# A three-block fp32 kernel on one core: the last stage's three products as half products, gated in SBUF

## The chip, the core and the metric

The kernel runs on one core of a Trainium2 chip. The metric is the device time of one execution in microseconds, from the runs of the kernel before: a median of 3840.6 over three runs (3840.37, 3840.6 and 3845.19).

## What is computed

Three residual blocks follow each other on 1024 rows of width 1024, all in fp32. The change lies at the end of the third one, and in the pools of the second and third. What matters of the reference:

```python
def hybrid_layer(x, w_in, ..., w_pa, w_pb, w_o):
    ...
    g_a = jax.nn.sigmoid(gate_a + b_gate[:D_MODEL])
    g_b = jax.nn.sigmoid(gate_b + b_gate[D_MODEL:])
    m = g_a * (y_a @ w_pa) + g_b * (y_b @ w_pb)
    return x + rms_norm_3(m @ w_o, g_post)
```

y_a is 1024 x 2048, y_b is 1024 x 1024, and all three results are 1024 x 1024. So the stage has three matrix products with inner sizes 2048, 1024 and 1024.

## The kernel before

Every fp32 operand is split into a high part, rounded by a copy on ACT (L183), and a low part, the difference taken on DVE (L184). A product of two operands is three matmuls: high by high, high by low, low by high (`mm3`, L266). A matmul is 128x128 by 128x512, and eight PSUM banks of 128x512 hold the results.

Two stages of the kernel already use fewer products. `Seven` (L1701) makes the third block's gates and first branch with seven products of quarter blocks in place of eight. `Second` (L2448) does the second block's second feed-forward product the same way: m = 1 to 7 are products of 512-column halves, each with an operand that is one block or a sum or difference of two. The A operands come ready from HBM (`hS`), since the stage ahead makes their sums; the B operands are weight blocks, summed on POOL (L2485). A product of one step is 24 matmuls (two k tiles, three matmuls each, four row tiles). After the last step each product's four 128x512 results are added to or taken from one or two quadrants of `xm`; products 1, 3, 4 and 5 go to SBUF by an ACT copy (L2513) and are added on DVE and POOL (L2517), the others from PSUM on DVE.

The last stage, `merge` (L2237), uses all eight: 384 matmuls for y_b @ w_pb (`from_b`, L2224), 768 for y_a @ w_pa, 384 for m @ w_o, 1536 in all. It goes through the two halves of the rows one after the other. `from_b` multiplies its result by the gate on DVE (L2233) and stores it to HBM (`mb`); `from_a` loads it again, multiplies its own result by the other gate (L2266), adds (L2267) and splits the sum for the last product. That one is squared on ACT for the norm (L2295), multiplied by g_post (L2296), scaled and added to x on DVE (L2305), and stored (L2306). The first two weight units of w_pb run inside `third_block` (L2612): one is woven into the end of Seven's gate units (`early`, L2643), one follows it.

Each engine works through its own instruction list in order, and DMAs issued by SP stand in one list as well. Tiles come from pools whose addresses are fixed; a load into a buffer waits for the last reader of what lay there. Operand tiles of 16 KB a partition come from a ring of six slots. In the third block, the pools `sum3`, `raw`, `ug` and `w2` lie one behind the other. In the second block, the raw blocks of the half products have 5 + 10 buffers of 4 KB (`f4`, `f4x`). mod (L2109) makes the heads of the third block, v_proj (L2118) follows it, with an activation table load on ACT between.

Of the kernel before, what the change touches and what calls it, by code (L numbers as in the profile page):

```python
# [1890 lines left out]
class Block3:  # L1891
# [331 lines left out]

    def from_b(self, u, hf, W, Ab, bank, new):  # L2224

        c, nc = self.c, self.c.nc
        hs = slice(512 * hf, 512 * hf + 512)
        for i in range(2):
            cc = 2 * u + i
            g = self.gate(1, cc, hs, new)  # L2230
# [4 lines left out]
            yield

    def merge(self, Ab, out, slot, tmp):  # L2237
# [3 lines left out]
        gp = c.bcast(ins["g_post_3"][0], tmp, 1024, "gpost")  # L2241
        mh = [slot.tile([128, 8, 512], R, name=t) for t in ("mhi", "mlo")]

        new = lambda: tmp.tile([128, 512], F32, tag="gt", name=c.nm("gt"), bufs=3)

        for hf in range(2):
            hs = slice(512 * hf, 512 * hf + 512)

            def rest_b():
                for u in range(2 - 2 * hf, 4):  # L2250
                    W = c.wunit([ins["w_proj_b_3"][0][:, 256 * u:256 * u + 256]])
                    yield from self.from_b(u, hf, W, Ab, "mm", new)

            def from_a(A):
                for u in range(4):
                    W = [c.wunit([ins["w_proj_a_3"][0][1024 * n:1024 * n + 1024, 256 * u:256 * u + 256]]) for n in range(2)]
                    for i in range(2):
                        cc = 2 * u + i
                        g = self.gate(0, cc, hs, new)
                        m = tmp.tile([128, 512], F32, tag="mb", name=c.nm("mb"), bufs=3)  # L2260
                        nc.sync.dma_start(m, self.mb[128 * cc:128 * cc + 128, hs])
                        q = c.psum("mm")
                        for n in range(2):
                            c.mm3(q, W[n], A[n], slice(128 * i, 128 * i + 128), slice(0, 512), [(k, k) for k in range(8)],
                                  first=n == 0, last=n == 1)
                        TT(g, g, q, op=OP.mult)  # L2266
                        TT(g, g, m, op=OP.add)  # L2267
                        c.split(mh[0][:, cc], mh[1][:, cc], g)

            Aa = [c.act_half(), c.act_half()]  # L2270
            load = chain(*(load_act(c, self.yaT[1024 * n:1024 * n + 1024], hf, Aa[n]) for n in range(2)))
            weave([(rest_b(), 4 + 4 * hf), (load, 8)])
            from_a(Aa)
            ys, xs = ([x[:, i] for i in range(4)] for x in (c.slot([128, 4, 1024], F32, "ys"), c.slot([128, 4, 1024], F32, "xs")))
            ms = tmp.tile([128, 4, 2], F32, tag="fms", name=c.nm("fms"), bufs=2)
            for i in range(4):
                t = 4 * hf + i
                nc.sync.dma_start(xs[i], self.x3[t * 128:t * 128 + 128])
            if hf == 0:
                Ab = c.act_half()  # L2280
                nextb = load_act(c, self.ybT, 1, Ab)
            for nh in range(2):
                ns = slice(512 * nh, 512 * nh + 512)
                q = []
                for kh in range(2):
                    W = c.wunit([ins["w_out_3"][0][512 * kh:512 * kh + 512, ns]], ktiles=4)
                    for i in range(4):
                        if kh == 0:
                            q.append(c.psum("mm"))
                        c.mm3(q[i], mh, W, slice(i * 128, i * 128 + 128), slice(0, 512), [(4 * kh + k, k) for k in range(4)],  # L2290
                              first=kh == 0, last=kh == 1)
                        if kh == 0:
                            continue
                        sq = tmp.tile([128, 512], BF, tag="fsq", name=c.nm("sq"), bufs=1)
                        nc.scalar.activation(sq, q[i], AF.Square, accum_out=ms[:, i, nh:nh + 1])  # L2295
                        TT(ys[i][:, ns], q[i], gp[:, ns], op=OP.mult)  # L2296
                    if hf == 0:
                        next(nextb, None)
            m = c.sm([128, 4])
            nc.vector.tensor_reduce(m, ms, axis=AX.X, op=OP.add)  # L2300
            rs = c.sm([128, 4])
            c.rsqrt(rs, m, 1.0 / D, 1e-6)
# [409 lines left out]
```

## Time and profile before

| | |
|---|---|
| median of three runs | 3840.6 us |
| the profiled execution's own time | 3843.21 us |
| its span | 3841.5 us |
| PE busy | 3648.8 us (95%) |
| DVE busy | 2319.5 us (60%) |
| ACT busy | 1388.2 us (36%) |
| POOL busy | 1157.4 us (30%) |
| last stage, from its first matmul to the end of the span | 3463.8 to 3841.5 us |

The times of the profile are of one execution, counted from the span's start. A row of the timeline gives an instruction's start, its length, its engine, its line, what it writes and reads, how many were put together (x4), and in square brackets how long the engine stood idle before it and what released it. A window row gives the busy time of each engine and the number of its instructions in the stretch. An engine counts as busy while an instruction of it is under way, also where that instruction is held up.

### The profile page before, as it was taken

Reading aid. Unit: us, or ns where it says so; the run is one execution under the profiler, and the core shown is the slowest. Engines: PE = TensorE matmul, PEld = TensorE weight load, DVE = VectorE, ACT = ScalarE, POOL = GpSimd, SP = SyncE. Lnnn points to the kernel's source line nnn. Section 1 sums busy time; section 2 is a strip of 40 time slices with the busy share of each in tenths; the row PEclk is TensorE's granted clock in tenths of the full one; section 3 lists DMA queues with packets and bytes.
Section 4 is the critical chain, followed back from the end, with each engine's and each line's share of the span. In section 5 each row is a group of like instructions: output and inputs, shape, how many; then the busy total and the mean of one; then the engine's idle time right before and its main releaser. Section 6 shows DMA issues by size and latency. Waiting matters only on the chain.

```text
span 3841.5 us, 53575 instructions
## 1 busy us (share of the span) xinstructions
PE 3648.8 (95%) x19640; PEld 3016.9 (79%) x19640; DVE 2319.5 (60%) x4641; ACT 1388.2 (36%) x2781; POOL 1157.4 (30%) x1342
## 2 busy tenths in 40 slices
PE   7999999899988999899899999999989999999998
PEld 6788888777877877688788888877778888887887
DVE  4456568758977856787667844444443666544443
ACT  5344435632234433322234533333322333332322
POOL 1011124400028731476446101211251655420000
PEclk9999998899998999999999999999999999999999
DMA  5321242342212135144685431111122333337462
GB/s 153 125 67 50 73 147 71 109 145 67 88 59 61 40 105 177 62 161 147 245 283 199 154 115 50 45 55 56 44 98 97 95 98 112 103 115 265 145 233 88
DMA packets 428954, 442.26 MB, mean 115 GB/s; under 512 B 58574, under 2 KB 309266, under 8 KB 428690
## 3 DMA queue, kind: packets, MB, share of 16 engines
q1 hardware_dynamic: 427458, 436.21, 35.1%
q8 instruction: 155, 2.54, 0.3%
q10 hardware_dynamic: 1088, 2.10, 0.2%
q14 instruction: 109, 0.89, 0.1%
q0 software_dynamic: 144, 0.52, 0.0%
HBM read 318.15 MB, written 115.87 MB: 113 GB/s over the span
## 4 chain that ended last, share of the span: by engine, by line
PE 56%; DVE 4%; POOL 3%; DMA 2%; issue 2%; ACT 1%; SPq 0%; DVEq 0%; ACTq 0%; POOLq 0%
PE mm L266 23%; PE b L1821 8%; PE mm L2506 7%; PE d L1821 5%; PE a L1821 5%; PE s L2000 2%; PE o L2022 1%; PE s L2192 1%; PE o L2074 1%; DMA wraw<-in_w_in_dram 0%; POOL v L1740 0%; DVE w L184 0%; PE t L2067 0%; DMA catT<-y 0%; POOL ws L1472 0%
## 5 line engine op out<-in xcount | busy, mean ns | idle before, releaser
L266 PE MATMUL mm<-ahi,whi 128*128 128x512 f32 x1408 | 557.6, 397 | 6.0 <-issue 3.7
L266 PE MATMUL mm<-alo,whi 128*128 128x512 f32 x1408 | 555.7, 395 | 1.6 <-DVE alo L223 1.6
L266 PE MATMUL mm<-ahi,wlo 128*128 128x512 f32 x1408 | 554.1, 394 | 0.4 <-DVE wlo L184 0.4
L266 PE MATMUL mm<-whi,ahi 128*128 128x512 f32 (+2 forms) x960 | 349.7, 370 | 30.5 <-ACT ahi L1660 10.1
L184 DVE TENSOR_TENSOR wlo<-wraw,whi 128x1024 fp32r<-128x1024 f32 (+2 forms) x200 | 246.8, 1268 | 193.7 <-PE mm L266 139.9
L266 PE MATMUL mm<-wlo,ahi 128*128 128x512 f32 (+2 forms) x960 | 352.3, 367 | 3.3 <-DVE wlo L184 3.3
L266 PE MATMUL mm<-whi,alo 128*128 128x512 f32 (+2 forms) x960 | 350.4, 366 | 0.3 <-DVE alo L223 0.3
L2506 PE MATMUL mm<-fop 128*128 128x512 f32 x1344 | 309.8, 392 | 10.7 <-ACT fop L183 10.7
L183 ACT ACTIVATE whi<-wraw 128x1024 fp32r<-128x1024 f32 (+2 forms) x200 | 202.4, 1057 | 321.6 <-DMA wraw<-in_w_in_dram 108.4
L266 PEld LDWEIGHTS mm<-ahi,whi 128*128 128x128 f32 x1408 | 268.1, 191 | 62.9 <-issue 4.5
L266 PEld LDWEIGHTS mm<-ahi,wlo 128*128 128x128 f32 x1408 | 267.1, 190 | 56.7 <-DVE wlo L184 1.9
L266 PEld LDWEIGHTS mm<-alo,whi 128*128 128x128 f32 x1408 | 267.3, 190 | 55.7 <-DVE alo L223 2.3
L2506 PEld LDWEIGHTS mm<-fop 128*128 128x128 f32 x1344 | 253.9, 189 | 64.0 <-ACT fop L183 11.2
L1821 PE MATMUL b<-sum,w 128*128 128x512 f32 x912 | 234.7, 400 | 4.0 <-DVE r L1871 3.8
L266 PEld LDWEIGHTS mm<-whi,ahi 128*128 128x128 f32 x960 | 183.4, 191 | 62.4 <-ACT ug L2133 10.5
L1821 PE MATMUL a<-ahi,w 128*128 128x512 f32 x656 | 223.8, 403 | 1.9 <-ACT r L1869 0.7
L266 PEld LDWEIGHTS mm<-wlo,ahi 128*128 128x128 f32 x960 | 183.4, 191 | 34.6 <-DVE wlo L184 4.6
L1821 PEld LDWEIGHTS b<-sum,w 128*128 128x128 f32 x912 | 171.7, 190 | 44.9 <-DVE r L1871 4.3
L266 PEld LDWEIGHTS mm<-whi,alo 128*128 128x128 f32 x960 | 183.1, 191 | 29.6 <-issue 2.5
L184 DVE TENSOR_TENSOR w<-T,w 128x512 fp32r<-128x512 f32 x152 | 143.0, 948 | 78.9 <-ACT w L183 78.5
L580 POOL TENSOR_SCALAR S<-S,sn 128x64 f32<-128x64 f32 (+8 forms) x96 | 56.6, 593 | 383.8 <-DVE sn L578 159.5
L1793 POOL TENSOR_TENSOR T<-raw 128x1024 f32<-128x1024 f32 x38 | 92.3, 2429 | 245.7 <-DMA gv<-ug 126.0
(654 smaller groups left out, 7690.4 us busy)
## 6 DMA issues: line engine op xcount, KB each, us to landing
f<-in_w_ff_dram SPq DMA_DIRECT2D x70, 512.0 KB
wraw<-in_w_in_dram SPq DMA_DIRECT2D x33, 1024.0 KB
f<-hS SPq DMA_DIRECT2D x54, 512.0 KB
wraw<-in_w_out_dram SPq DMA_DIRECT2D x24, 1024.0 KB
raw<-in_w_in_dram SPq DMA_DIRECT2D x96, 256.0 KB
hS<-sc SPq DMA_DIRECT2D x80, 256.0 KB
raw<-in_w_ff_dram SPq DMA_DIRECT2D x64, 256.0 KB
wraw<-in_w_proj_a_dram SPq DMA_DIRECT2D x16, 1024.0 KB
```

The source lines that it names most:

```text
L183: nc.scalar.activation(hi, src, AF.Copy)
L184: nc.vector.tensor_tensor(lo, src, hi.bitcast(F32), op=OP.subtract)
L266: nc.tensor.matmul(out, lhs[a][:, kl, ls], rhs[b][:, kr, rs], start=first and n == 0, stop=last and n == tot - 1)
L580: nc.gpsimd.tensor_scalar(S_[:, :n], S_[:, :n], r, 1.0, op0=OP.mult, op1=OP.mult)
L1793: G = lambda o, a, b: nc.gpsimd.tensor_tensor(o, a, b, op=OP.subtract)
L1821: self.c.nc.tensor.matmul(o, w[:, i, k], A[j][:, k], start=first and m == 0, stop=m == 11, skip_group_check=True)
L2000: nc.tensor.matmul(q[:, :256], qk[:, a, qcol], qk[:, b, kcol], start=n == 0, stop=n == 2)
L2022: nc.tensor.matmul(ob[:, 128 * (b % 4):128 * (b % 4 + i1 - i0)], vt[:w, cc + 1], pt[:, 128 * i0:128 * i1], start=b % 4 == 0 and cc == b - ...
L2074: nc.tensor.matmul(o[:, 256 * (r % 2):256 * (r % 2) + 256], vg[:, r, kb], pt[:, 256 * kb:256 * kb + 256], start=kb == 0, stop=kb == 1)
L2192: nc.tensor.matmul(q[:, 128 * t:128 * t + 128], self.vl[:, 4 * hf + t], self.wt, start=True, stop=True)
L2506: nc.tensor.matmul(q[m, t], o[m][:, a, k, 128 * t:128 * t + 128], o[m][:, 2 + b, k], start=s == 0 and n == 0, stop=s == 7 and n == 5)
```

## The change

`Second` becomes a general half-product machine: it gets functions for the blocks of A and of B, the number of steps, the result tiles and the order of its groups. A sums are made on DVE, B sums on POOL. `drive` runs a list of such items, always preparing one item ahead, and calls a function behind chosen items. `Raws` hands out the buffers of raw blocks in turn.

`merge` is three of these: B (w_pb, y_b; 2 steps), A (w_pa, y_a; 4 steps) and O (m, w_out; 2 steps), 56 products of 24 matmuls, 1344 in all. The results are transposed halves in SBUF: `Cb` in a pool, `Ca` in two ring slots, which leaves four slots for operands. The first value of a quadrant is written by an ACT copy. B is gated on POOL, A on DVE and added to B there (`gate_b`, `gate_a`); O reads its A operand from `Ca` directly. `finish` squares on ACT, multiplies by g_post on POOL and does the last multiply-add on DVE, with x and the output in the two buffers that the gates used. Nothing of the stage runs inside Seven any more.

```diff
-    def merge(self, Ab, out, slot, tmp):
+    def merge(self, f4, pool, out):
...
+        raws = Raws(c, [(f4, 4)], 4)
...
+            raws.use([(f4, 4), (fx, 6)])
+            Ca = [c.slot([128, 4, 1024], F32, "ca") for _ in range(2)]
+            Cb = [cp.tile([128, 4, 1024], F32, name=c.nm("cb")) for _ in range(2)]
+            order = [(7, 5), (4, 1), (3, 6), (2,)]
...
+            O = Second(c, lambda x, s: Ca[j(x)][:, 2 * s:2 * s + 2, 512 * i(x):512 * i(x) + 512],
+                       raws.block(wo, j, lambda x, s: 512 * i(x) + 256 * s), 2, Cb, [(3, 6), (7, 5), (4, 1), (2,)], True)
+            items = B.items + A.items + O.items
+            full = lambda t: gp.tile([128, 1024], F32, tag="gt", name=c.nm(t), bufs=2)
...
+            def gate_b():
+                for h in range(2):
+                    for t in range(4):
+                        nc.gpsimd.tensor_tensor(Cb[h][:, t], Cb[h][:, t], gate(1, h, t), op=OP.mult)
+
+            def gate_a(h):
+                for t in range(4):
+                    TT(Ca[h][:, t], Ca[h][:, t], gate(0, h, t), op=OP.mult)
+                    TT(Ca[h][:, t], Ca[h][:, t], Cb[h][:, t], op=OP.add)
...
+            def finish(h):
...
+                    nc.scalar.activation(sq, Cb[h][:, t], AF.Square, accum_out=ms[:, 4 * h + t:4 * h + t + 1])
+                    nc.gpsimd.tensor_tensor(Cb[h][:, t], Cb[h][:, t], gpost, op=OP.mult)
...
+                for t in range(4):
+                    x = full("xr")
+                    r = 512 * h + 128 * t
+                    nc.sync.dma_start(x, self.x3[r:r + 128])
+                    nc.vector.scalar_tensor_tensor(x, Cb[h][:, t], rs[:, 4 * h + t:4 * h + t + 1], x, op0=OP.mult, op1=OP.add)
+                    nc.sync.dma_start(out[r:r + 128], x)
+
+            nb, na = len(B.items), len(A.items)
+            after = {nb - 1: gate_b, nb + 11: lambda: gate_a(0), nb + na - 1: lambda: gate_a(1), len(items) - 3: lambda: finish(0),
+                     len(items) - 1: lambda: finish(1)}
+            for _ in drive(items, ta, tb, ep, after):
+                pass
...
 class Second:
+    A = {1: (11, 22, OP.add), 2: (21, 22, OP.add), 3: (11,), 4: (22,), 5: (11, 12, OP.add), 6: (21, 11, OP.subtract),
+         7: (12, 22, OP.subtract)}
...
+            t = p.tile([128, 2, 512], F32, tag="ft", name=c.nm("ft"), bufs=2)
+            eng.tensor_tensor(t, raw[f, spec[0]], raw[f, spec[1]], op=spec[2])
...
+            b = operand(self.b, self.B[m], tb, nc.gpsimd, m)
+            a = operand(self.a, self.A[m] if ta else (m,), ta, nc.vector, m)
+            c.split(o[:, 0], o[:, 1], a)
             c.split(o[:, 2], o[:, 3], b)
...
+    def add(self, m, t, ep):
...
+        if m != 2 and len(old) == 2:
+            e = ep.tile([128, 512], F32, tag="fe", name=c.nm("fe"), bufs=4)
+            nc.scalar.activation(e, self.q[m, t], AF.Copy)
+        for j, (x, plus) in enumerate(self.C[m]):
+            d = self.Cs[x // 10 - 1][:, t, 512 * (x % 10 - 1):512 * (x % 10)]
+            if x in self.new:
+                nc.scalar.activation(d, self.q[m, t], AF.Copy)
+            else:
+                eng = nc.gpsimd if j and m != 2 and len(old) == 2 else nc.vector
+                eng.tensor_tensor(d, d, e, op=OP.add if plus else OP.subtract)
```

The pools move as well. In the second block the raw buffers are 4 + 11. In the third, `raw` lies first, then `sum3`, `w2` and `ug`, and the first four raw blocks of `merge`, loaded from ACT's queue, lie where `raw` was:

```diff
-                sec.raws = [(f4, 5)] * 5 + [(fx, 10)] * 10
+                raws.use([(f4, 4), (fx, 11)])
...
+            rp = enter("raw")
             seven = Seven(c, X, enter("sum3"))
-            rp = enter("raw")
             seven.rp = rp
+            w2 = enter("w2")
             ug = enter("ug")
...
-            w2 = enter("w2")
...
+    with pool("f4") as f4:
+        b.merge(f4, pool, out)
```

The order of instructions is set by a scheduler from the code, so three places of it follow.

The end of DVE's list, in the kernel before: the last steps of the reciprocal root (L166 to L168) and the four multiply-adds with x.

```order
L168 SCALAR_TENSOR_TENSOR s4_5469_32572<-s4_5470_32573,s4_5469_32572 128x4
L166 TENSOR_TENSOR s4_5470_32573<-s4_5469_32572 128x4
L167 TENSOR_TENSOR s4_5470_32573<-s4_5470_32573,s4_5468_32571 128x4
L168 SCALAR_TENSOR_TENSOR s4_5467_32570<-s4_5470_32573,s4_5469_32572 128x4
L2305 SCALAR_TENSOR_TENSOR xs_5436_32306<-ys_5435_32305,s4_5467_32570,xs_5436_32306 128x1024 x4
```

And in the changed kernel, where L2494 is an addition of a product (mm: from PSUM) and L2275 the multiply-add with x:

```order
L2494 TENSOR_TENSOR cb_5230_30349<-cb_5230_30349,mm_5618_32702 128x512 x2
L168 SCALAR_TENSOR_TENSOR frs_30352<-s4_5608_32651,s4_5607_32650 128x4
L2494 TENSOR_TENSOR cb_5230_30349<-cb_5230_30349,mm_5619_32709 128x512 x2
L2275 SCALAR_TENSOR_TENSOR xr_5609_32663<-cb_5229_30348,frs_30352,xr_5609_32663 128x1024
L2275 SCALAR_TENSOR_TENSOR xr_5610_32667<-cb_5229_30348,frs_30352,xr_5610_32667 128x1024
L159 TENSOR_SCALAR s4_5624_32760<-fms_30351 128x4
```

The multiply-adds of the first half (cb_5229) stand behind the additions of the last product; mm_5619 is its last tile. Six more follow behind the second reciprocal root.

The end of SP's list, in the kernel before: the loads of the last weights, and the four stores.

```order
L238 DMA wraw_5438_32312<-in_w_out_3_dram 128x4x512
L238 DMA wraw_5445_32372<-in_w_out_3_dram 128x4x512
L238 DMA wraw_5452_32440<-in_w_out_3_dram 128x4x512
L238 DMA wraw_5459_32500<-in_w_out_3_dram 128x4x512
L2306 DMA out_0_dram<-xs_5436_32306 128x1024 x4
```

In the changed kernel (f4 is a raw block of w_out):

```order
L2523 DMA f4_5614_32680<-in_w_out_3_dram 128x2x512
L2274 DMA xr_5609_32663<-x3_14599 128x1024
L2274 DMA xr_5610_32667<-x3_14599 128x1024
L2276 DMA out_0_dram<-xr_5609_32663 128x1024
L2276 DMA out_0_dram<-xr_5610_32667 128x1024
L2274 DMA xr_5611_32671<-x3_14599 128x1024
L2274 DMA xr_5612_32675<-x3_14599 128x1024
L2276 DMA out_0_dram<-xr_5611_32671 128x1024
```

The loads of x, all early before, now alternate in pairs with the stores; two more such pairs follow.

The seam of A and O on DVE. In the kernel before, the corresponding place is the end of `from_a`, where g and m make the operand of the last product:

```order
L2266 TENSOR_TENSOR gt_5432_32248<-gt_5432_32248,mm_5434_32252 128x512
L184 TENSOR_TENSOR wlo_5447_32374<-wraw_5445_32372,whi_5446_32373 128x1024
L2267 TENSOR_TENSOR gt_5432_32248<-gt_5432_32248,mb_5433_32250 128x512
L184 TENSOR_TENSOR mlo_30510<-gt_5432_32248,mhi_30509 128x512
L184 TENSOR_TENSOR wlo_5454_32442<-wraw_5452_32440,whi_5453_32441 128x1024 x2
```

In the changed kernel, L2254 and L2255 are gate_a's multiply and add on `Ca`, L2452 is an operand sum, fop_5545 holds the operands of O's first product 7, and fop_5550 those of its first product 5:

```order
L184 TENSOR_TENSOR fop_5545_32231<-ft_5548_32236,fop_5545_32231 128x1024
L2254 TENSOR_TENSOR ca_5228_30347<-ca_5228_30347,gt_5527_32145 128x1024
L2255 TENSOR_TENSOR ca_5228_30347<-ca_5228_30347,cb_5230_30349 128x1024
L2254 TENSOR_TENSOR ca_5228_30347<-ca_5228_30347,gt_5528_32149 128x1024
L2255 TENSOR_TENSOR ca_5228_30347<-ca_5228_30347,cb_5230_30349 128x1024
L2452 TENSOR_TENSOR ft_5549_32238<-ca_5228_30347 128x1024
L2452 TENSOR_TENSOR ft_5551_32245<-ca_5227_30346,ca_5228_30347 128x1024
L2255 TENSOR_TENSOR ca_5228_30347<-ca_5228_30347,cb_5230_30349 128x1024
L2494 TENSOR_TENSOR cb_5230_30349<-cb_5230_30349,mm_5541_32203 128x512
L2494 TENSOR_TENSOR cb_5230_30349<-cb_5230_30349,mm_5542_32210 128x512
L2494 TENSOR_TENSOR cb_5230_30349<-cb_5230_30349,mm_5543_32217 128x512
L184 TENSOR_TENSOR fop_5545_32231<-ft_5549_32238,fop_5545_32231 128x1024
```

Ahead of these rows stand two more operations of gate_a on the same half (L2254, L2255), and ahead of those the low parts of O's second step. So the gates of the second half lie between the operands of O's second and third item.

## Rows read from the trace of the kernel before

**Rows 1.** The page: span; busy us, share and instructions of each engine.

```profile
span 3841.5 us, 53575 instructions
PE 3648.8 (95%) x19640; PEld 3016.9 (79%) x19640; DVE 2319.5 (60%) x4641; ACT 1388.2 (36%) x2781; POOL 1157.4 (30%) x1342
```

**Rows 2.** Windows: length, busy us (x) by engine, PEclk, DMA share, GB/s.

```profile
3650.00:3700.00 50.00, 50.00 (x222) 41.39 (x221) 29.66 (x41) 13.66 (x16) 0.00 (x0) 1.00 0.74 260
```

**Rows 3.** ACT timeline, second block: start, us, what, [idle before <-releaser].

```profile
1956.86 1.06 ACT L183 ACTIVATE fop<-f 128x1024 fp32r<-128x1024 f32 x1 [3.43 <-PE mm L2506]
1962.30 1.06 ACT L183 ACTIVATE fop<-f 128x1024 fp32r<-128x1024 f32 x1 [3.43 <-PE mm L2506]
```

**Rows 4.** PE timeline: the last stage's first rows, Seven's end, last matmul.

```profile
3463.81 0.40 PE L266 MATMUL a<-ahi,wx 128*128 128x512 f32 x1
...
3469.18 0.40 PE L1821 MATMUL b<-ahi,w 128*128 128x512 f32 x1
...
3474.78 0.40 PE L266 MATMUL a<-ahi,wx 128*128 128x512 f32 x1
...
3827.41 0.39 PE L266 MATMUL mm<-whi,mlo 128*128 128x512 f32 x1
```

**Rows 5.** DVE and POOL timelines, second block; POOL alone in Seven.

```profile
2075.30 1.22 DVE L184 TENSOR_TENSOR fop<-f,fop 128x1024 fp32r<-128x1024 f32 x1
2076.44 3.41 DVE L184 TENSOR_TENSOR fop<-ft,fop 128x1024 fp32r<-128x1024 f32 x1
2079.77 1.21 DVE L184 TENSOR_TENSOR fop<-f,fop 128x1024 fp32r<-128x1024 f32 x1
...
2058.42 7.93 POOL L2517 TENSOR_TENSOR xm<-xm,fe 128x512 f32<-128x512 f32 x4
2075.46 3.31 POOL L2485 TENSOR_TENSOR ft<-f,f 128x1024 f32<-128x1024 f32 x1 [2.90 <-DVE fop L184]
...
3390.67 2.40 POOL L1793 TENSOR_TENSOR T<-raw 128x1024 f32<-128x1024 f32 x1 [14.47 <-DVE w L184]
```

**Rows 6.** DVE and POOL timelines: PSUM and SBUF operands beside POOL.

```profile
3394.60 0.68 DVE L1871 TENSOR_TENSOR r<-r,b 128x512 f32<-128x512 f32 x1
3395.20 1.17 DVE L184 TENSOR_TENSOR w<-T,w 128x512 fp32r<-128x512 f32 x1
...
3393.15 2.67 POOL L1793 TENSOR_TENSOR T<-raw,T 128x512 f32<-128x512 f32 x2
```

**Rows 7.** Windows as in rows 2: second block's half products.

```profile
2050.00:2100.00 50.00, 50.00 (x222) 41.40 (x222) 49.57 (x26) 22.95 (x27) 39.37 (x16) 1.00 0.59 195
```

**Rows 8.** DVE and SP timelines: the end of the kernel.

```profile
3831.59 4.87 DVE L2305 SCALAR_TENSOR_TENSOR xs<-ys,s,xs 128x1024 f32<-128x1024 f32 x4
...
3836.49 0.33 SPq L2306 DMA_DIRECT2D out_dram<-xs  x1
```

**Rows 9.** SP and DVE timelines: store then load; load then reader.

```profile
3506.74 0.32 SPq L2234 DMA_DIRECT2D mb<-gt  x1
3508.80 0.32 SPq L2221 DMA_DIRECT2D gt<-gT  x1
...
3485.54 0.32 SPq L2221 DMA_DIRECT2D ug<-gT  x1
...
3488.50 0.69 DVE L2233 TENSOR_TENSOR ug<-ug,a 128x512 f32<-128x512 f32 x1 [1.01 <-DMA ug<-gT]
```

**Rows 10.** Timeline: from the last mixed head to v_proj.

```profile
2786.70 1.08 DVE L2106 SCALAR_TENSOR_TENSOR yb<-dd,zb 128x512 f32<-128x512 f32 x1
...
2791.85 1.28 ACT L2133 ACT_TABLE_LOAD   x1 [8.91 <-DMA ybT<-yb]
...
2793.80 0.79 PE L266 MATMUL mm<-whi,ahi 128*128 128x512 f32 x1 [9.67 <-ACT ug L2133]
```

**Rows 11.** ACT and PE timelines: hidden layer to half products.

```profile
1881.85 1.06 ACT L183 ACTIVATE fop<-f 128x1024 fp32r<-128x1024 f32 x1 [4.42 <-DMA f<-hS]
...
1882.96 1.65 PE L2506 MATMUL mm<-fop 128*128 128x512 f32 x3 [10.75 <-ACT fop L183]
```

More of the change, by code (lines that the diff above doesn't have):

```diff
@@ L2237, in merge @@
-    def merge(self, Ab, out, slot, tmp):
+    def merge(self, f4, pool, out):
         c, nc, ins = self.c, self.c.nc, self.c.ins
         TT = nc.vector.tensor_tensor
[L2241 to L2302, printed above, removed]
-            for i in range(4):
-                t = 4 * hf + i
-                nc.vector.scalar_tensor_tensor(xs[i], ys[i], rs[:, i:i + 1], xs[i], op0=OP.mult, op1=OP.add)
-                nc.sync.dma_start(out[t * 128:t * 128 + 128], xs[i])
@@ new lines, in parts, with operand @@
+    def parts(self, group, s, ta, tb):
+        c, nc = self.c, self.c.nc
+        out, raw = {}, {}
+        def operand(f, spec, p, eng, m):
+            for x in spec[:2]:
+                if (f, x) not in raw:
+                    raw[f, x] = f(x, s)
+            if len(spec) == 1:
+                return raw[f, spec[0]]
+            t = p.tile([128, 2, 512], F32, tag="ft", name=c.nm("ft"), bufs=2)
+            eng.tensor_tensor(t, raw[f, spec[0]], raw[f, spec[1]], op=spec[2])
+            return t
+        for m in group:
+            o = out[m] = c.slot([128, 4, 2, 512], R, "fop")
+            b = operand(self.b, self.B[m], tb, nc.gpsimd, m)
+            a = operand(self.a, self.A[m] if ta else (m,), ta, nc.vector, m)
+            c.split(o[:, 0], o[:, 1], a)
@@ new lines, in products @@
+    def products(self, g, s, o, ep):
+        c, nc, q = self.c, self.c.nc, self.q
+        for m in g:
+            for t in range(4):
+                if s == 0:
+                    q[m, t] = c.psum("mm")
+                n = 0
+                for k in range(2):
+                    for a, b in ((0, 0), (0, 1), (1, 0)):
+                        nc.tensor.matmul(q[m, t], o[m][:, a, k, 128 * t:128 * t + 128], o[m][:, 2 + b, k],
+                                         start=s == 0 and n == 0, stop=s == self.steps - 1 and n == 5)
+                        n += 1
+                if s == self.steps - 1:
+                    self.add(m, t, ep)
+            if s == self.steps - 1:
+                self.new -= {x for x, _ in self.C[m]}
+            yield
@@ new lines, in add @@
+    def add(self, m, t, ep):
+        nc, c = self.c.nc, self.c
+        e = self.q[m, t]
+        old = [x for x, _ in self.C[m] if x not in self.new]
+        if m != 2 and len(old) == 2:
[8 more added lines that the diff above has]
+                eng.tensor_tensor(d, d, e, op=OP.add if plus else OP.subtract)
@@ new lines, in drive, with __init__, use, __call__ @@
+def drive(items, ta, tb, ep, after={}):
+    made = [items[0][0].parts(*items[0][1:], ta, tb)]
+    for i, (sec, g, s) in enumerate(items):
+        if i + 1 < len(items):
+            made.append(items[i + 1][0].parts(*items[i + 1][1:], ta, tb))
+        yield from sec.products(g, s, made[i], ep)
+        made[i] = None
+        if i in after:
+            after[i]()
+class Raws:
+    def __init__(self, c, places, n=0):
+        self.c, self.n, self.early = c, 0, n
+        self.use(places)
+    def use(self, places):
+        self.places = [(p, n) for p, n in places for _ in range(n)]
+    def __call__(self, src):
+        p, bufs = self.places[self.n % len(self.places)]
+        self.n += 1
+        t = p.tile([128, 2, 512], F32, tag="f4", name=self.c.nm("f4"), bufs=bufs)
+        (self.c.nc.scalar if self.n <= self.early else self.c.nc.sync).dma_start(t, src)
+        return t
+    def block(self, w, half, rows):
+        return lambda x, s: self(w[rows(x, s):rows(x, s) + 256, 512 * half(x):512 * half(x) + 512].rearrange(
+            "(k p) n -> p k n", p=128))
```

138 lines of the change are left out of this document (38 added, 100 removed).

## The prediction

> **What bounds the kernel now.** I read the page first. TensorE is busy for 95% of the span and no other engine above 60% [rows 1]. Then a window inside the last stage: in 50 us PE is busy for 50.00 us, with 222 matmuls at full clock, DVE for 29.66, POOL for nothing [rows 2]. So the stage lasts as long as its matmuls, and POOL and some 40% of DVE are free. The price of a matmul comes from the second block, where the same half products already run: ACT gets a freed operand slot every 1962.30 − 1956.86 = 5.44 us [rows 3], one product of 24 matmuls, 0.2267 us each.
>
> Then PE's timeline for the stage's ends [rows 4]. The first stage matmul starts at 3463.81; it and its 23 neighbours lie inside Seven, up to 3469.18, and Seven's own last matmul hands over at 3474.78. Without those 5.37 us Seven would end at T0 = 3469.4. The last matmul ends at 3827.8. The old stage is thus worth 358.4 us after T0: 1536 × 0.2267 = 348.2 and some 10 of waits and lower clock.
>
> **The change, part by part.**
>
> *Matmuls.* B has 2 steps, A 4, O 2, each of 7 products: 56 × 24 = 1344, 192 fewer. 56 × 5.44 = 304.6 us after T0 if nothing waits. This is 43.5 us less than 348.2, and all on the path.
>
> *Start.* The first operands lie in buffers that are free early. The second product needs a raw block in a new buffer, whose load stands on SP behind the last gate store, some 4 us after T0 by my estimate. Then a load (a 256 KB load took 3488.50 − 3485.54 = 2.96 [rows 9]; 512 KB some 0.65 more), a sum and a low part of 1.14 each [rows 5] and ACT's 1.06 [rows 3], about 11 in all: a gap of near 5 after the first product's 5.44, and 2 for a lower clock behind it. **7 us**; bounds 3 and 14.
>
> *DVE against POOL.* Each step's operands now cost DVE sums and low parts, and POOL sums, all 128x1024 between SBUF tiles. Rows 5 show such a pair: DVE's operations start 1.14 apart when alone, but the one that meets POOL's sum lasts 3.41, and the next starts 3.33 later. POOL's sum, 2.40 alone, lasts 3.31. They take turns: 1.14 per DVE and 2.19 per POOL operation. An addition with a PSUM operand is not held (0.68 beside POOL, against 1.17 for the SBUF pair behind it [rows 6]). So I add up turns. Groups (7,5): 6 DVE and 1 POOL, 9.0 us; (4,1) and (3,6): 5 and 2, 10.1 each; (2): 3 and none, 3.4; PE takes 10.88 for the pairs and 5.44 for the last. The additions of product 3 go to both engines, four each; beside each other four took 7.93 [rows 5], so 8.
> - B: 2 × (9.0 + 10.1 + 10.1 + 3.4) + 8 = 73 against 76.2 on PE. Twenty-four PSUM additions (16 us of DVE) fit only in part beside POOL. Loss **2** (0 to 5).
> - A up to its last (3,6): 4 × 29.2 = 117, and gate_b's eight POOL multiplies 17.5, make 134 against 130.6, with PSUM additions on top; four operand slots give a lead of under three products. Loss **9** (3 to 18).
> - A into O: DVE's order decides it (the rows of the seam in the section on the change). O cannot multiply before m is gated. The first four products of O just about keep up: I find 2 to 3 us lost. But between the low parts of O's second step and those of its product 7 stand, in DVE's order, seven of gate_a(1)'s eight operations, two operand sums and three PSUM additions: with product 7's own two low parts eleven turns of 1.14, one POOL sum and 1.8, 16.5 us, where PE has 5.44 of work. Loss there 11, at the seam **14** (6 to 24).
> - The rest of O: **2** (0 to 5).
>
> Together 27 us of waits inside the stage, bounds 9 and 52.
>
> The Trainium skill, "SBUF — State Buffer", section "Who interferes with whom", states that a DVE instruction with two SBUF inputs contends with a GpSimd instruction that reads SBUF, and that the loser is blocked for the whole instruction. Rows 5 agree with it in the 2.27 us that were added; by that rule the turns above are a floor for the stage, whatever DVE's share of time says. Against the sum speaks one row: in a window of the same half products, with DVE counted busy 49.57 of 50 and POOL 39.37, PE lost nothing [rows 7]. If that held here, the 27 would be near 5. But that window has neither operand sums on DVE nor gates, so I keep 27 and give the other its own case.
>
> *Tail.* Now DVE ends with four operations of 1.28 in a row, their inputs loaded long before, and the last output store is issued 0.03 us after them; the span ends 5.0 us after DVE [rows 8]. That makes 3841.5 − 3827.8 = 13.7 after PE. In the changed kernel the first final multiply-add stands in DVE's order behind the last PSUM additions, and x and the output share two 128x1024 buffers. So eight tiles go through as four pairs, all after PE: multiply-add, store, then the next load into the same buffer. A 256 KB store held the load behind it for 3508.80 − 3506.74 = 2.06 us, and a load took 2.96 [rows 9]; with 0.65 for twice the bytes each, a turn is 1.28 + 2.7 + 3.6 = 7.6. The additions end 1.7 after PE; three turns 22.7; the last pair 2.6; then 5.0: 32 after PE, **18 more than now**. Below: 5.4 per turn gives +12; above: 9 gives +22. POOL's last multiplies by g_post and the second rsqrt end 7 to 8 us after PE, inside the first turn.
>
> *Upstream.* The table load before v_proj waited for the ybT store until 2791.85, 4.1 us after the DVE result that it follows ended [rows 10]; in the new layout it waits for engines alone: **−4** (−6 to 0). Before the second block's half products PE stood 10.75 us, the last part for loads into buffers that were still in use [rows 11]; four of the raw buffers are now free earlier: **−3.5** (−10 to 0).
>
> *At nothing.* The mb round trip through HBM goes, its loads were hidden. ACT takes 56 × 2.1 of high parts and, by my estimate, some 36 of copies, about half of the stage. Loads are some 126 of 0.5 MB, 200 GB/s over the stage, less than the 260 moved beside a full PE in rows 2.
>
> *Sum.* 3469.4 + 7 + 304.6 + 27 + 32 − 7.5 = 3832.5 against a span of 3841.5: −9. The profiled execution took 3843.2; the median of the runs, 3840.6, lies 2.6 below it. On the median: **3832**.
>
> **The rivals.**
> - *PE stays the bound.* Turns and seam cost 5 instead of 27. For: rows 7. Against: the turns of rows 5 are too many by addition alone. 3832 − 22 = 3810.
> - *Slower: the DVE–POOL pair becomes the bound of A and O.* PSUM additions never overlap, gate_b falls into A's first groups undiluted, and the seam costs its 24: 52 of waits, 3857. It decides from 36 us of waits on, where the gain is gone; 44 can be measured. For: A's ledger is already over PE's time. Against: POOL's gates stand in pairs between sums in its order, and its sums run ahead.
> - *The tail is short*: stores and loads turn in 5.4 us. For: these are the smaller transfers' own times. Against: twice the bytes, and both directions in flight. 3826.
> - *The upstream savings do not show*, because another wait ends at the same place: 3839.
>
> **How the numbers follow.** My forecast with waits of 15 to 36 us (3820 to 3841) has 0.53, the tail and upstream cases in it; PE as the bound 0.22; the slower rival 0.25. A measurement of this kernel tells 0.2%, 7.7 us, from no change. Faster by more needs waits under 28 or so: 0.22 + 0.28 = 0.50. Slower by more needs waits over 44: 0.19. The rest, 0.31, is within it. The range reaches from the PE-bound case with the shorter tail, 3804, to the slower rival, 3858; a tenth is left out on each side.
>
> **What would show it.** Right: 1344 stage matmuls; PE full at 222 per 50 us in B; DVE operations of over 3 us beside POOL's sums in A; PE's longest wait of the stage at O's first product 7, for a low part; the last PE matmul near 3801 and eight multiply-adds in pairs some 7.6 us apart behind it. Wrong: no PE wait inside the stage (the first rival); waits spread over all of A (the second); multiply-adds before the last matmul.

## The result and the profile after

The changed kernel took 3888.0 us (median of four runs, 3881.8 to 3893.2) beside 3842.9 of the kernel before on the same chip: a ratio of 1.0111 [1.0097, 1.0124]. A second set gave 3883.0 beside 3843.8, 1.0094 [1.0073, 1.0116]. So it is slower by about 1%, where 3832 us was forecast.

The profiled execution took 3881.8 us, its span 3880.1. This is the head of its page of the profile, which answers to [rows 1]:

```profile
span 3880.1 us, 53463 instructions
...
PE 3623.0 (93%) x19448; PEld 2991.6 (77%) x19448; DVE 2505.5 (65%) x4715; ACT 1434.1 (37%) x2833; POOL 1371.5 (35%) x1414
```

PE has its 192 matmuls less and is busy for 25.8 us less; DVE has 186 us more, POOL 214. No engine but PE is near full over the span, so the page alone does not say why the kernel is slower. Four marks of the timeline cut the span into pieces: the hidden layer's first matmul of the second block (L1821), Seven's end without stage matmuls (T0), the end of the last matmul, and the end.

| us | before | after | forecast |
|---|---|---|---|
| first block, to the hidden layer's first matmul | 1528.2 | 1536.1 | 1528.2 |
| from there to T0 | 1941.2 | 1938.2 | 1933.7 |
| T0 to the end of the last matmul | 358.4 | 358.1 | 338.6 |
| last matmul to the end | 13.7 | 47.7 | 32 |
| span | 3841.5 | 3880.1 | 3832.5 |

The stage has an eighth fewer matmuls and lasts as long as it did; the tail takes 34 us more. The stage's matmuls, in the view of groups by line and form for the stretch 3474.3 to 3833 (count, then busy us and mean ns, then idle time and what ended it):

```profile
L2472 PE MATMUL mm<-fop 128*128 128x512 f32 x1344 | 322.4, 402 | 35.6 <-ACT fop L183 12.6 <-DVE cb L2494 10.9 <-DVE ca L2494 7.9
```

1344 matmuls at the 0.2267 us of [rows 3] are 304.6 us. The stage lasted 358.1, so 53.5 were lost: 35.5 of waits, and 18 in which PE was at work, but slower. PE's timeline of the stage shows both (all rows in which it waited; x is the number of matmuls up to the next wait):

```profile
3476.02 4.83 PE L2472 MATMUL mm<-fop 128*128 128x512 f32 x20 [0.62 <-DVE fop L184]
3487.02 9.16 PE L2472 MATMUL mm<-fop 128*128 128x512 f32 x32 [6.17 <-ACT fop L183]
3497.22 31.12 PE L2472 MATMUL mm<-fop 128*128 128x512 f32 x136 [1.04 <-ACT fop L183]
3530.36 2.15 PE L2472 MATMUL mm<-fop 128*128 128x512 f32 x6 [2.02 <-ACT cb L2491]
3533.93 36.48 PE L2472 MATMUL mm<-fop 128*128 128x512 f32 x150 [1.42 <-ACT cb L2491]
3570.59 3.03 PE L2472 MATMUL mm<-fop 128*128 128x512 f32 x12 [0.18 <-DVE cb L2494]
3584.38 46.55 PE L2472 MATMUL mm<-fop 128*128 128x512 f32 x192 [10.76 <-DVE cb L2494]
3633.66 111.31 PE L2472 MATMUL mm<-fop 128*128 128x512 f32 x480 [2.73 <-DVE ca L2494]
3745.26 1.63 PE L2472 MATMUL mm<-fop 128*128 128x512 f32 x6 [0.28 <-DVE ca L2494]
3751.80 17.48 PE L2472 MATMUL mm<-fop 128*128 128x512 f32 x66 [4.91 <-DVE ca L2494]
3774.65 57.72 PE L2472 MATMUL mm<-fop 128*128 128x512 f32 x240 [5.37 <-ACT fop L183]
```

In us, the waits are 7.8 at the start, 3.6 in B, 10.8 at the start of A, 2.7 in A's middle and 10.6 at the seam into O (5.37 of it at O's first product 7). Take the stretch behind the longest wait: 192 matmuls should take 43.5 us and took 46.55, 3.0 more. Behind the waits of 6.17, 2.73, 4.91 and 5.37 it is 1.9, 2.5, 2.5 and 3.3, and behind the pair of 2.02 and 1.42 it is 3.3 in all. The windows show why (three of 20 us, then two of 2 us; columns as in [rows 2]):

```profile
3560.00:3580.00 20.00, 13.45 (x58) 10.45 (x57) 18.64 (x11) 5.19 (x5) 20.00 (x9) 0.89 0.63 209
3580.00:3600.00 20.00, 15.49 (x57) 12.28 (x58) 20.00 (x16) 4.02 (x4) 14.28 (x6) 0.77 0.70 246
3600.00:3620.00 20.00, 20.00 (x90) 16.58 (x89) 18.32 (x11) 10.45 (x12) 12.00 (x4) 1.00 0.74 253
...
3586.00:3588.00 2.00, 2.00 (x7) 1.52 (x6) 2.00 (x1) 0.00 (x0) 1.71 (x1) 0.50 0.65 249
...
3596.00:3598.00 2.00, 2.00 (x11) 1.65 (x10) 2.00 (x2) 0.00 (x0) 2.00 (x1) 1.00 0.93 331
```

The granted clock is 1.00 in the third slice, where PE doesn't wait (2.4 GHz), and 0.77 on average in the one with the end of the longest wait. The short windows part the two levels: just behind the wait the clock is 0.50 (1.2 GHz) and 2 us hold 7 matmuls, ten us later it is 1.00 and 2 us hold 11. It fell where PE stood, and came back with work. The slices of 20 us with the other waits have 0.83, 0.83, 0.91, 0.83 and 0.84. Some 2 of the 18 are only the last matmul of each stretch, whose end counts 0.40 in place of 0.2267.

What makes PE wait 10.76 at the start of A? It wants a PSUM bank that an addition on DVE (L2494, the four from 3583.05) has to empty. DVE's timeline, then POOL's:

```profile
3571.06 2.23 DVE L184 TENSOR_TENSOR fop<-ft,fop 128x1024 fp32r<-128x1024 f32 x1
3573.20 3.37 DVE L184 TENSOR_TENSOR fop<-f,fop 128x1024 fp32r<-128x1024 f32 x1
3576.49 3.36 DVE L184 TENSOR_TENSOR fop<-ft,fop 128x1024 fp32r<-128x1024 f32 x1
3579.77 3.36 DVE L2452 TENSOR_TENSOR ft<-f,f 128x1024 f32<-128x1024 f32 x1
3583.05 2.47 DVE L2494 TENSOR_TENSOR cb<-cb,mm 128x512 f32<-128x512 f32 x4
...
3568.82 6.67 POOL L2250 TENSOR_TENSOR cb<-cb,gt 128x1024 f32<-128x1024 f32 x2
3575.45 6.60 POOL L2452 TENSOR_TENSOR ft<-f,f 128x1024 f32<-128x1024 f32 x2
3582.01 5.70 POOL L2250 TENSOR_TENSOR cb<-cb,gt 128x1024 f32<-128x1024 f32 x2
```

POOL runs without a break: gates (L2250), sums (L2452), gates. A DVE operation that meets one of POOL's from its start lasts 3.36 in place of 1.2, as in [rows 5], and the next starts 3.28 behind it. Four of them stand ahead of the additions; alone they would have taken 4.6 us, here they took 12.

The tail, DVE's timeline and then POOL's (the last matmul ended at 3832.4):

```profile
3830.92 1.82 DVE L159 TENSOR_SCALAR s<-fms 128x4 f32<-128x4 f32 x1 [1.71 <-ACT sq L2267]
3832.78 2.27 DVE L160 TENSOR_SCALAR s<-s 128x4 int32<-128x4 int32 x1
3835.08 2.26 DVE L166 TENSOR_TENSOR s<-s 128x4 f32<-128x4 f32 x1
3837.37 2.26 DVE L167 TENSOR_TENSOR s<-s,s 128x4 f32<-128x4 f32 x1
3839.66 0.16 DVE L168 SCALAR_TENSOR_TENSOR s<-s,s 128x4 f32<-128x4 f32 x1
...
3845.22 1.27 DVE L2494 TENSOR_TENSOR cb<-cb,mm 128x512 f32<-128x512 f32 x2
3846.42 5.53 DVE L2275 SCALAR_TENSOR_TENSOR xr<-cb,frs,xr 128x1024 f32<-128x1024 f32 x2
...
3856.62 1.28 DVE L2275 SCALAR_TENSOR_TENSOR xr<-cb,frs,xr 128x1024 f32<-128x1024 f32 x1 [0.47 <-DMA xr<-x]
...
3864.67 1.29 DVE L2275 SCALAR_TENSOR_TENSOR xr<-cb,frs,xr 128x1024 f32<-128x1024 f32 x1 [4.68 <-DMA xr<-x]
...
3872.94 1.28 DVE L2275 SCALAR_TENSOR_TENSOR xr<-cb,frs,xr 128x1024 f32<-128x1024 f32 x1 [4.57 <-DMA xr<-x]
...
3830.34 9.28 POOL L2268 TENSOR_TENSOR cb<-cb,gpost 128x1024 f32<-128x1024 f32 x4
```

The first five rows are steps of the reciprocal root on 128x4 values. Alone such a step takes 0.16 us (the fifth). While POOL multiplies by g_post (L2268), each of the first four waits for one of POOL's four operations and takes up to 2.27. They stand in DVE's order ahead of the last additions, which so end 14 us behind the last matmul. Then come the four pairs of multiply-adds, 10.2, 8.1 and 8.3 apart, the last three waiting for x. SP's rows of the second turn, the two stores and then the two loads into the same buffers:

```profile
3857.93 2.43 SPq L2276 DMA_DIRECT2D out_dram<-xr  x2
...
3860.56 2.72 SPq L2274 DMA_DIRECT2D xr<-x  x2
```

The first load is issued 2.6 behind the first store, and its reader on DVE starts 4.1 behind that.

### The profile page after: what moved, and what is told of

It reads as the page before. It is cut to its first block, busy times and chain, and to the rows that moved or that the text cites. A ratio compares the mean times of both kernels' runs of the same rounds, so it can differ in the third digit from the quotient of the medians.

```text
span 3880.1 us, 53463 instructions
## 1 busy us (share of the span) xinstructions
PE 3623.0 (93%) x19448; PEld 2991.6 (77%) x19448; DVE 2505.5 (65%) x4715; ACT 1434.1 (37%) x2833; POOL 1371.5 (35%) x1414
## 3 DMA queue, kind: packets, MB, share of 16 engines
q1 hardware_dynamic: 417954, 445.65, 35.5%
## 5 line engine op out<-in xcount | busy, mean ns | idle before, releaser
L2472 PE MATMUL mm<-fop 128*128 128x512 f32 x2688 | 635.7, 398 | 43.0 <-ACT fop L183 20.0
L2472 PEld LDWEIGHTS mm<-fop 128*128 128x128 f32 x2688 | 515.9, 193 | 159.6 <-ACT fop L183 22.1
L266 PE MATMUL mm<-ahi,whi 128*128 128x512 f32 x1056 | 418.4, 398 | 2.8 <-ACT ahi L221 2.6
L266 PE MATMUL mm<-alo,whi 128*128 128x512 f32 x1056 | 416.4, 395 | 1.3 <-DVE alo L223 1.3
L266 PE MATMUL mm<-ahi,wlo 128*128 128x512 f32 x1056 | 415.5, 394 | 0.4 <-DVE wlo L184 0.4
L266 PE MATMUL mm<-whi,ahi 128*128 128x512 f32 (+2 forms) x960 | 350.4, 370 | 28.7 <-ACT ahi L1660 10.1
L2452 POOL TENSOR_TENSOR ft<-f,f 128x1024 f32<-128x1024 f32 x80 | 242.3, 3031 | 274.7 <-DVE fop L184 171.4
L184 DVE TENSOR_TENSOR wlo<-wraw,whi 128x1024 fp32r<-128x1024 f32 (+1 forms) x140 | 174.9, 1284 | 119.1 <-PE mm L266 96.0
L1821 PE MATMUL b<-sum,w 128*128 128x512 f32 x912 | 235.2, 400 | 3.1 <-DVE r L1871 2.9
L1821 PE MATMUL a<-ahi,w 128*128 128x512 f32 x656 | 223.4, 402 | 1.5 <-ACT r L1869 0.7
L184 DVE TENSOR_TENSOR fop<-ft,fop 128x1024 fp32r<-128x1024 f32 x120 | 205.9, 1728 | 18.6 <-ACT fop L183 18.5
L1821 PEld LDWEIGHTS b<-sum,w 128*128 128x128 f32 x912 | 171.6, 190 | 44.1 <-DVE r L1871 3.3
L183 ACT ACTIVATE whi<-wraw 128x1024 fp32r<-128x1024 f32 (+1 forms) x140 | 142.1, 1059 | 166.7 <-DMA wraw<-in_w_in_dram 105.8
L184 DVE TENSOR_TENSOR fop<-f,fop 128x1024 fp32r<-128x1024 f32 x100 | 153.5, 1548 | 75.6 <-ACT fop L183 66.2
```

The lines of the kernel that those rows point to most:

```text
L183: nc.scalar.activation(hi, src, AF.Copy)
L184: nc.vector.tensor_tensor(lo, src, hi.bitcast(F32), op=OP.subtract)
L266: nc.tensor.matmul(out, lhs[a][:, kl, ls], rhs[b][:, kr, rs], start=first and n == 0, stop=last and n == tot - 1)
L1821: self.c.nc.tensor.matmul(o, w[:, i, k], A[j][:, k], start=first and m == 0, stop=m == 11, skip_group_check=True)
L2452: eng.tensor_tensor(t, raw[f, spec[0]], raw[f, spec[1]], op=spec[2])
L2472: nc.tensor.matmul(q[m, t], o[m][:, a, k, 128 * t:128 * t + 128], o[m][:, 2 + b, k], start=s == 0 and n == 0, stop=s == self.steps - 1 and ...
```

## The experiments

Two theories stood against each other. By the first, POOL's operations cost more by the turns that they take from DVE than they spare it; by the rival, DVE is simply too full, or the loads are late, and POOL's help is a gain. Every execution brings its own first block (1523.7 to 1538.7 us for the same instructions), so kernels that were executed only once (e1, e3, e5 to e8) are compared by the stage (T0 to the last matmul's end) and the tail.

**The sums of the weight operands on DVE (e1_sums).**

```diff
-            b = operand(self.b, self.B[m], tb, nc.gpsimd, m)
+            b = operand(self.b, self.B[m], tb, nc.vector if ta else nc.gpsimd, m)
```

> The B operand sums of the last stage go from POOL to DVE, nothing else. Theory 1 (DVE and POOL take turns on 128x1024 SBUF operations, 1.14 and 2.19 us each): 40 sums cost 1.14 in place of 2.19, so 42 us of turns go; PE's waits inside the stage fall from 35.5 us to 15 to 25, and the loss to a lower clock behind them from 18 to about 10; the span falls to 3850 to 3865. Theory 2 (DVE itself is the bound, its list being too long): 40 more operations on DVE cost 46 us; PE's waits grow to 60 or more, span over 3900. Theory 3 (the waits come from DMA or PSUM banks): waits stay within 30 to 40, span 3875 to 3885.

Time 3844.5, span 3842.8; stage 340.0, tail 43.8. PE's rows with waits over 1 us:

```profile
3472.00 77.93 PE L2472 MATMUL mm<-fop 128*128 128x512 f32 x336 [7.42 <-ACT fop L183]
3554.58 13.93 PE L2472 MATMUL mm<-fop 128*128 128x512 f32 x48 [4.65 <-ACT fop L183]
3571.67 150.38 PE L2472 MATMUL mm<-fop 128*128 128x512 f32 x650 [3.16 <-ACT fop L183]
...
3739.50 3.12 PE L2472 MATMUL mm<-fop 128*128 128x512 f32 x6 [5.67 <-ACT fop L183]
```

DVE makes POOL's 40 sums as well, and the stage became 18 us shorter: waits 22.2 in place of 35.5. Behind the wait ahead of its second product, B runs to its end without one, and A's first product too. The span fell by 37 us, but 12 of those are a first block that was shorter in this execution, and 3 lie between it and T0; the sums are worth 18 in the stage and 4 in the tail.

**All of the stage's POOL work on DVE (e2_nopool).** Beside the sums, gate_b, the multiply by g_post and the copied additions:

```diff
-                        nc.gpsimd.tensor_tensor(Cb[h][:, t], Cb[h][:, t], gate(1, h, t), op=OP.mult)
+                        TT(Cb[h][:, t], Cb[h][:, t], gate(1, h, t), op=OP.mult)
...
-                eng = nc.gpsimd if j and m != 2 and len(old) == 2 else nc.vector
+                eng = nc.gpsimd if j and m != 2 and len(old) == 2 and self.steps == 8 else nc.vector
```

> As the run before, and gate_b, the second additions of product 3 and the multiplies by g_post go to DVE too, so POOL does nothing in the last stage. Theory 1: no DVE operation of the stage lasts over 1.4 us, additions in the tail are no longer held up (they ended 14 us after the last matmul, now 3 to 6), waits of PE 8 to 18, span 3825 to 3845. Theory 2: waits over 60 us, span over 3900. Theory 3: as changed kernel, waits 30 to 40.

Median 3838.4 of ten runs beside 3845.7 of thirteen of the kernel before; ratio 0.9981 [0.9970, 0.9993]. Stage 327.1, tail 39.1, waits 14.3. In the groups by line and form (3475 to 3830), the two largest of DVE:

```profile
L184 DVE TENSOR_TENSOR fop<-ft,fop 128x1024 fp32r<-128x1024 f32 x78 | 94.4, 1238 | 8.7 <-ACT fop L183 8.7
L2452 DVE TENSOR_TENSOR ft<-f,f 128x1024 f32<-128x1024 f32 x68 | 82.0, 1232 | 13.3 <-DMA f<-in_w_proj_b_dram 9.0 <-DMA f<-in_w_proj_a_dram 3.0 <-DMA f<-in_w_out_dram 1.1
```

In the changed kernel the same two had means of 1618 and 1678 ns; POOL's sums 3261. A sum costs DVE 1.23 us if it makes it itself, and over 2 if POOL makes it beside DVE's work. The rival falls: DVE does all of POOL's work and PE waits less.

**The x tiles in raw buffers (e3_tail).** x and the output go to eight buffers that are free by then, so the loads come early.

```diff
-                    x = full("xr")
...
-                    nc.sync.dma_start(x, self.x3[r:r + 128])
+                    x = raws(self.x3[r:r + 128].rearrange("p (a b) -> p a b", a=2)).rearrange("p a b -> p (a b)")
```

> The changed kernel with x and the output in raw buffers (ten, long free) in place of two shared ones; POOL's work stays. If the turns of store and load set the end, the six loads between the multiply-adds (12.6 us of DVE idle before them) go: eight multiply-adds stand in a row, some 5 us of the wait is replaced by POOL's multiplies by g_post, and the span falls by 10 to 15, to 3865 to 3870. If DVE's late additions alone set the end, it falls by under 4.

Time 3859.5, span 3857.7; stage 358.5, unchanged, tail 35.1, 12.6 less. DVE's rows:

```profile
3836.71 10.01 DVE L2274 SCALAR_TENSOR_TENSOR f<-cb,frs,f 128x1024 f32<-128x1024 f32 x4
...
3848.87 4.87 DVE L2274 SCALAR_TENSOR_TENSOR f<-cb,frs,f 128x1024 f32<-128x1024 f32 x4
```

No multiply-add waits for a load any more. The first four still meet POOL's second round of g_post (10.01 in place of 4.87), and they still begin 14.1 behind the last matmul, which ended at 3822.6. The span fell by more than the 10 to 15 expected, 22.4, but the other 10 are a first block 6.6 shorter and a stretch from there to T0 3.5 shorter, which this edit doesn't touch. (Lines behind L2271 are one less here and in e4_all.)

**Both together (e4_all):** the edits of e2_nopool and e3_tail.

> POOL empty in the last stage and x in raw buffers, both together. Theory 1: stage waits 8 to 18 us as in the second run, and after the last matmul additions, gates by g_post, root and eight multiply-adds on DVE alone, near 17 us, then 5 to the end: span 3810 to 3828, below the 3841.5 of before. Theory 2: over 3890.

Median 3820.8 (3817.4 to 3823.9) beside 3845.7; ratio 0.9930 [0.9914, 0.9946]: faster than both kernels. Stage 327.3, tail 22.9. PE's rows with waits over 0.9:

```profile
3479.56 78.44 PE L2471 MATMUL mm<-fop 128*128 128x512 f32 x338 [7.49 <-ACT fop L183]
...
3561.88 0.74 PE L2471 MATMUL mm<-fop 128*128 128x512 f32 x2 [1.00 <-DVE cb L2493]
...
3729.46 9.31 PE L2471 MATMUL mm<-fop 128*128 128x512 f32 x26 [3.13 <-DVE fop L184]
```

What is left is the start and the seam, and 1.6 at the start of A. The tail is still 9 us longer than before: DVE was busy for all 20 us of the slice in which PE ends, and additions, multiplies and roots of the last tiles follow it.

**The second block's buffers alone (e5_raws)**, in the kernel before:

```diff
-                sec.raws = [(f4, 5)] * 5 + [(fx, 10)] * 10
+                sec.raws = [(f4, 4)] * 4 + [(fx, 11)] * 11
...
-            sec.raws = [(f4, 5)]
+            sec.raws = [(f4, 4)]
```

> The kernel before with the raw blocks of the second block in 4 + 11 buffers as the change has them, the old load order and the old last stage. In the changed kernel the first matmul behind the half products of the second block came 6.5 us later than before. If the buffers do this (first product hoisted ahead of the hidden layer's last results, whose stores then come later), the step from hidden to half products ends 4 to 7 us later, span 3845 to 3849. If the load order alone does it, no change within 1.5 us, span 3840 to 3843.

Time 3850.9 beside 3853.0. PE's waits at the place of [rows 11]:

```profile
1883.47 8.19 PE L2506 MATMUL mm<-fop 128*128 128x512 f32 x24 [3.85 <-ACT fop L183]
1897.48 7.75 PE L2506 MATMUL mm<-fop 128*128 128x512 f32 x23 [5.82 <-ACT fop L183]
```

The wait of 10.75 became two of 3.85 and 5.82, behind the first and the second product. Counted from the hidden layer's first matmul, the last half product ended after 672.3 us in place of 672.5: no gain, and none of the 4 to 7 us of delay that these buffers were thought to make. The first product starts earlier, and the loads that the third one needs come later, since they stand on SP behind the hidden layer's last stores: these were issued until 1886.2 in place of 1877.0, of which 3.1 is the longer first block. (The span, 3849.2, is 7.7 longer than before, but for other reasons: besides those 3.1, the stretch from the half products to v_proj, with the same instructions in nearly the same order, took 6.8 more.)

**The third block's pool order alone (e6_pools)**, in the kernel before:

```diff
+            rp = enter("raw")
             seven = Seven(c, X, enter("sum3"))
-            rp = enter("raw")
             seven.rp = rp
+            w2 = enter("w2")
...
-            w2 = enter("w2")
```

> The kernel before with the third block's pools in the new order (raw, sum3, w2, ug), old last stage. If the table load ahead of v_proj is freed by this order, the wait of 9.67 us before v_proj falls to 5 to 6; in the changed kernel a second wait of 2.7 us appeared in v_proj; if that belongs to the order too, the first matmul of Seven (2963.4 before) comes 1 to 2 us earlier, else 4 us earlier. Span 3836 to 3841.

Time 3847.6. The row of [rows 10]:

```profile
2798.24 0.80 PE L266 MATMUL mm<-whi,ahi 128*128 128x512 f32 x1 [5.68 <-ACT ug L2133]
```

The wait fell from 9.67 to 5.68, the 4 us forecast. A second wait behind it grew from 1.79 to 2.74. From the end of the last matmul ahead of the place (2792.6, before 2784.1) to the third block's first L1821 (2968.6, before 2963.4) it took 176.1 in place of 179.3. Of 4 us 3.2 remained. The span, 3845.9, is above the 3836 to 3841 expected; its first block alone was 6.3 longer.

**Only the multiply by g_post on DVE (e7_gpost).**

```diff
-                    nc.gpsimd.tensor_tensor(Cb[h][:, t], Cb[h][:, t], gpost, op=OP.mult)
+                    TT(Cb[h][:, t], Cb[h][:, t], gpost, op=OP.mult)
```

> The changed kernel with only the eight multiplies by g_post moved from POOL to DVE. In the changed kernel four steps of the first reciprocal root, each on 128x4 values, lasted 1.8 to 2.3 us beside those multiplies, and the last PSUM additions, which stand behind them on DVE, ended 14 us after the last matmul. If the turns hold small operations too, the four steps fall to 0.2 us, the additions end 3 to 7 us after the last matmul, and the time from the last matmul to the end of the span falls from 47.7 to 36 to 42. If the additions are late for another reason (DVE's list is simply full), they still end 11 or more after it. Waits inside the stage unchanged, 33 to 37.

Time 3872.2, span 3870.5; stage 358.3, tail 44.7. The root's first steps and the first pair:

```profile
3828.26 0.16 DVE L159 TENSOR_SCALAR s<-fms 128x4 f32<-128x4 f32 x1
3828.45 0.17 DVE L160 TENSOR_SCALAR s<-s 128x4 int32<-128x4 int32 x1
...
3839.18 2.48 DVE L2275 SCALAR_TENSOR_TENSOR xr<-cb,frs,xr 128x1024 f32<-128x1024 f32 x2
```

The steps take 0.16 again, so it was g_post on POOL that held them. The tail gained only 3 us, less than expected: the additions ended 10.1 behind the last matmul in place of 14, since four of the multiplies now stand ahead of them on DVE and two between them, and the pairs still turn through two buffers.

**Only gate_b on DVE (e8_gateb).**

```diff
-                        nc.gpsimd.tensor_tensor(Cb[h][:, t], Cb[h][:, t], gate(1, h, t), op=OP.mult)
+                        TT(Cb[h][:, t], Cb[h][:, t], gate(1, h, t), op=OP.mult)
```

> The changed kernel with only gate_b's eight multiplies moved from POOL to DVE. If gate_b between POOL's sums makes the longest wait of the stage (10.8 us, first step of A, behind DVE's last additions of B), that wait falls under 4 and the stage gets 10 to 18 us shorter with its lower clock (358 from its first matmul to its last in the changed kernel, so 340 to 348). If the additions of product 3 on both engines make it, it stays over 8 and the stage over 352.

Time 3880.1, stage 353.8. PE's rows at the start of A and in its middle:

```profile
3580.43 45.80 PE L2472 MATMUL mm<-fop 128*128 128x512 f32 x192 [2.06 <-DVE cb L2494]
3630.55 111.99 PE L2472 MATMUL mm<-fop 128*128 128x512 f32 x480 [4.32 <-DVE ca L2494]
```

The wait of 10.76 is down to 2.06, so POOL's gates made it. But the stage is only 4.3 shorter, not the 10 and more expected: the waits fell by 4.9 in all (30.6), since B and A's middle wait 1.6 longer each and O's last products 1.1, and the lower clock cost as much as before.

**The changed kernel again (e9_again).**

> The changed kernel itself once more. In its profiled execution the hidden layer's first matmul, ahead of which nothing was changed, came 7.9 us later than in the kernel before; kernels with the same code up to there put it between 1523.7 and 1536.1 us. If that is a difference between executions and not of the change, it lies within 1523 to 1537 here, and the ratio to the kernel before is smaller than the 1.0111 measured, 1.006 to 1.010. If it belongs to the change, the matmul comes at 1534 or later again and the ratio stays at 1.010 to 1.012.

The ratio is given above. The same waits stand at the same places (10.77 at the start of A, 4.91 and 5.33 at the seam), the stage took 358.2, the tail 48.3, and the first block 1533.9. So stage and tail are the change's. The first block and the ratio of 1.0094 fit the first case, in which the block's length belongs to the execution; but at 1533.9 it lies only 0.1 below the bound of the second, so this run by itself hardly tells the two apart. The stretch from there to T0 did not repeat: it took 1944.9 in place of 1938.2, more than the 1941.2 of the kernel before.

## Why the prediction was wrong

It gave slower by over 0.2% a chance of 0.19, and the result lies 30 us above the end of the range. The slower rival came nearest, but not by its own reasons. POOL's gates did fall on the start of A, but DVE and POOL did not bound A (480 matmuls of it ran without a wait), and its 52 us of waits were not there: the 35.5 measured are near the forecast's 32. What the forecast lacked, the clock behind the waits and the longer tail, no rival had either. Step by step:

- **What bounds before, and the matmuls: right.** 1344 matmuls, 304.6 us at full clock; the stretch of 480 took 111.3 against 108.8.
- **Turns: right in size.** 3.28 between DVE operations that meet POOL, against 1.14 + 2.19 forecast. The rule of the Trainium skill that was weighed there ("SBUF — State Buffer", "Who interferes with whom") held: the DVE operation is blocked for the whole of POOL's. The row that spoke against it, [rows 7], held for the 480 matmuls of A's later part, where PE lost nothing beside sums on both engines; it did not hold at the gates, at the seam and at the start of A.
- **Waits: nearly right in sum, wrong in place.** Forecast 27 inside the stage and about 5 at the start; measured 35.5. That the sum is near is in part luck: A lost 13.5 and not 9, the start 7.8 and not 5, the seam 10.6 and not 14, the rest of O nothing and not 2. The wait at O's first product 7 came, but with 5.37 in place of 11, not as the longest, and it ended with a high part from ACT, not with a low one. The start of A cost 10.76 at one spot: the prediction spread A's loss over its products by adding turns, and didn't follow which DVE operations stand ahead of the additions that free PE's banks.
- **The clock behind the waits: the first step that failed.** "2 for a lower clock" was set for the start and nothing for the other waits. Measured were 18 us in which PE worked below 304.6's pace, some 2 of them the ends of stretches; in the windows behind the longest wait the clock stood at 0.50. The other kernels agree (stage less 304.6 less waits): 18.6 beside waits of 30.6 (e8), 13.2 beside 22.2 (e1), 8.6 beside 14.1 (e4), 8.1 beside 14.3 (e2). That is 0.5 to 0.6 us for each us waited. No run changed the clock alone, so the rate is a reading of five kernels, not a test by itself.
- **The tail: the second step that failed.** "The additions end 1.7 after PE": they ended 14 after it. The root's 128x4 steps stand ahead of them and were held by POOL: four of them took 8.7, where 0.8 would do. The other 4.5 are, as an estimate from the same rows, DVE's own lateness: without the hold, too, all eight additions of the last product were still to be made when PE ended. The prediction saw that POOL's multiplies end late and called them hidden in the first turn; it counted turns for 128x1024 operations alone. e7 shows that hold, and e3 the buffers: with both removed (e4) the tail is 22.9. Three turns of the pairs took 26.5 in place of 22.7: the first was longer by the held multiply-adds (5.53 for two), and in the second the store held the load for 2.6 and the load took 4.1, where the sum has 2.7 and 3.6. No row shows the 0.65 that both of these contain for twice the bytes. Together 47.7 in place of 32.
- **Upstream: −3.0 in place of −7.5, and not clear of chance.** The half products ended 1.4 us earlier, not 3.5: the wait went, and others came up there (e5). The wait before v_proj fell by the 4 us forecast, of which 2.0 remained at the third block's first L1821 (177.3 in place of 179.3) and 3.2 in e6. What ends v_proj's second wait was not tried. Seven took 1.8 longer up to T0. And by its second execution (e9) the same stretch is 3.7 longer than before, not 3.0 shorter: between the half products and v_proj it took 8.4 us more than in the first, with the same instructions in the same order.
- **The first block: 8 us that no step had, and most likely chance.** Its instructions stand in the same order in both kernels, and its length varied by 15 us over the profiled executions; the three with the old last stage (before, e5, e6) average 1531.3, the eight with the new one 1532.0. Stage, tail and upstream make 31 us of the change; the medians differ by 39 to 45. Where the rest comes from stays open.

The misses on the span add up: 3.5 of waits, 16 of slower matmuls, 15.7 of tail, 4.5 upstream and 7.9 of the first block, 47.6 in all.

The change's own idea was sound. With the same half products and POOL left out, the stage falls from 358.4 to 327.3 us. What it lost, it lost by its division of work and by its buffers.

## What to carry to other kernels

Where DVE is the engine that others wait for, an operation given to POOL is not taken off DVE: here each meeting cost DVE 2.1 us of standing, where DVE makes the same sum in 1.23, and a 128x4 step is held as long as a 128x1024 one. Price a wait of PE with the slower matmuls behind it, here half as much again, and look for it in DVE's order at the operations ahead of those that free a PSUM bank. At the end of a kernel, inputs that are known early get buffers of their own, so that no load stands behind a store.

## What the runs showed of the hardware

Operations of DVE on 128x4 values went from 0.16 to as much as 2.27 us beside POOL, those with one SBUF tensor (L159, L160) like those with two (L167). The Trainium skill, "SBUF — State Buffer", section "Who interferes with whom", names the operation of a tensor with a scalar among those that can contend with GpSimd. The 1.82 and 2.27 us of L159 and L160 agree with it. The granted clock fell in each of the stage's waits of 2.7 to 10.8 us and behind the pair of 2.02 and 1.42 (slices of 0.77 to 0.91), in a kernel whose mean clock is 0.957.
